# A feed-forward layer with two plain blocks in place of four and ten Strassen pairs in place of nine, the first pair's weights prepared ahead of the token sums

## The chip, the cores and the metric

The kernel runs on one core of one Trainium2 chip. The metric is the device time in microseconds (us) of one execution. Before the change the median of three runs is 1004.85 us (1004.83 to 1004.9). The rows below come from one further execution that was taken with a profile: it took 1005.55 us, of which 1003.8 us lie between the first and the last instruction (its span).

## The reference

One decoder layer for 576 tokens of width 1024: 512 tokens of a prompt and 64 of eight short samples. A mixing part (convolution, recurrence and attention to a memory, joined by gates) comes first; the change is in the feed-forward part behind it, whose inner width D_FF is 2816:

```python
h = _rmsnorm(x, norm_pre_ffn)
f = jax.nn.silu(jnp.einsum('bld,df->blf', h, w_ffn_gate)) * jnp.einsum('bld,df->blf', h, w_ffn_up)
f = jnp.einsum('blf,fd->bld', f, w_ffn_down)
x = x + _rmsnorm(f, norm_post_ffn)
```

All inputs and outputs are fp32, and the result is wanted close to fp32 accuracy.

## The kernel before

**Three matmuls for one product.** Every operand of a product is split into a high and a low part (`split`, L99: the high part is a rounded copy by ScalarE on L102, or L105 where a scale goes with it; the low part is the difference, by VectorE on L103 or L106). `mm3` (L93) then issues three TensorE matmuls, high by high (L95), high by low (L96), low by high (L97). So each weight and each activation costs one instruction of ScalarE and one of VectorE before TensorE can use it.

**The feed-forward part** handles the 2816 inner columns as 22 blocks of 128 columns. `h2` holds the normalised tokens, high and low, as 8 blocks of 128 rows (the k blocks, along the 1024 of the width) by 576 tokens. `ffn_norm(ti)` writes it for one token tile: PE turns four blocks at a time into one PSUM bank (L1179), then ACT and DVE split each (L105, L106, 128x128 each). Token tiles 0 and 1 (tokens 0 to 255) come last. The next steps are:

- `ffn_group(f, w, g)` (L1197), a *plain* block: for block f and token group g (0: tokens 0 to 255; 1: tokens 256 to 575) 8 x 3 matmuls for the gate and as many for the up weights, each with a PSUM bank of its own; ACT's sigmoid (L1201) and two DVE multiplications (L1202, L1204) empty the banks. The two groups have 256 and 320 columns.
- `sprep(m)` and `smul(m, nxt)`, the *Strassen pairs*: two neighbouring blocks (256 columns) at once, as a 2 x 2 matrix of half width by half columns times a 2 x 2 matrix of half width by half tokens (288 each). Seven products in place of eight: 7 x 4 x 3 = 84 matmuls of 288 columns for the gate (m even) and as many for the up weights (m odd).
- The pairs need sums of the tokens: `token_sums_a` (L1223, tokens 288 to 575) and `token_sums_b` (L1232 for tokens 0 to 287, then L1234, L1236, L1237 and L1240 and four splits of 1152 elements; T0 to T3 are the split sums).
- They need sums of the weights too: `sprep(m)` loads 1 MB of raw weights (L1252) into one half of a ring of two, splits the quarter `a` (wa), makes four sums of 512 elements (L1269, L1270, L1276, L1277) and splits them and the quarters b and d (wq, 1024 elements each). `sprep` is a generator: each `next` goes to the following `yield`.
- The down projection follows behind the last pair.

**What sets the order.** The kernel is traced in program order, and the framework then orders each engine's queue by a simulation of its own; an engine works its queue strictly as it stands. Weights loaded by `ffn_w` (L1194) come from SP's queue, as do the raw weights and the write-back of the residual to DRAM (`spill`, L1358). PSUM gives four banks named mm and four named sd; a product can begin only when a bank of its name is free. With `LEAD = 4`, blocks 0 to 3 are plain and blocks 4 to 21 are nine pairs (m = 0 to 17). Blocks 0 and 1 are done for group 1, then `token_sums_a`, then blocks 0 and 1 for group 0, then `token_sums_b`, then blocks 2 and 3; `sprep(0)` is begun in block 3.

Of the kernel before, what the change touches and what calls it, by code (L numbers as in the profile page):

```python
# [27 lines left out]

WARM = 14

LEAD = 4

HELD = (2, 5)

# [8 lines left out]
def tile_decoder_layer(  # L43
# [19 lines left out]
    def nm(s):  # L63
        seq[0] += 1
        return f"{s}_{seq[0]}"

    def big(dt=F32, n=4608):
        return pS.tile([P, n], dt, tag="S", name=nm("S"))
# [7 lines left out]
    def mtmp(n=576, dt=F32):  # L76
        return pt.tile([P, n], dt, tag="mt", name=nm("mt"), bufs=2)
# [13 lines left out]
    def f32(ap):  # L91
        return ap.bitcast(F32)
# [6 lines left out]
    def split(hi, lo, src, scale=None, eng=None):  # L99

        if scale is None:
            A.activation(hi, src, AF.Copy)  # L102
            (eng or V).tensor_tensor(lo, src, f32(hi), op=ALU.subtract)  # L103
        else:
            ins = A.activation(hi, src, AF.Identity, scale=scale)  # L105
            ins2 = V.scalar_tensor_tensor(out=lo, in0=src, scalar=scale, in1=f32(hi), op0=ALU.mult,  # L106
                                          op1=ALU.subtract)
            return ins, ins2

    def wprep(src, k, c, hi=None, lo=None, eng=None):  # L110
        raw = pw.tile([P, k, c], F32, tag="wr", name=nm("wr"), bufs=3)
        nc.sync.dma_start(raw, src.rearrange("(k p) c -> p k c", p=P))
        if hi is None:
            hi = pw.tile([P, k, c], FR, tag="wh", name=nm("wh"), bufs=3)
            lo = pw.tile([P, k, c], FR, tag="wl", name=nm("wl"), bufs=3)
        split(hi, lo, raw, eng=eng)
        return hi, lo

    def proj(w, col, act, b0, nk, groups=(0, 1)):

        res = []
        whi, wlo = w
        ahi, alo = act
        for g in groups:
            t0, n = GRP[g]
            ps = mmb()
            for k in range(nk):
                mm3(ps[:, :n], whi[:, k, col:col + P], wlo[:, k, col:col + P],
                    ahi[:, b0 + k, t0:t0 + n], alo[:, b0 + k, t0:t0 + n], k == 0, k == nk - 1)
            res.append((ps, t0, n))  # L130
        return res
# [160 lines left out]
    def wcols(w, c, n=P):  # L292
        return w[0][:, c:c + n], 8 if w.shape[1] == D else w.shape[1] // P, n
# [895 lines left out]
    def hid(f):  # L1189
        while len(hids) <= f // 8:  # L1190
            hids.append(big().rearrange("p (f t) -> p f t", f=8))
        return hids[f // 8][:, f % 8]

    def ffn_w(f, eng=None):  # L1194
        return tuple(wprep(*wcols(w, P * f), eng=eng) for w in (w_ffn_gate, w_ffn_up))

    def ffn_group(f, w, g):  # L1197
        hf = hid(f)
        (ps, t0, n), = proj(w[0], 0, h2, 0, 8, (g,))
        sg = mtmp(320)  # L1200
        A.activation(sg[:, :n], ps[:, :n], AF.Sigmoid)  # L1201
        V.tensor_tensor(sg[:, :n], ps[:, :n], sg[:, :n], op=ALU.mult)  # L1202
        (ps, t0, n), = proj(w[1], 0, h2, 0, 8, (g,))
        V.tensor_tensor(hf[:, t0:t0 + n], ps[:, :n], sg[:, :n], op=ALU.mult)  # L1204
# [21 lines left out]
    def tsplit(i, src):  # L1226
        split(xT["hl"][0][:, i], xT["hl"][1][:, i], src)

    def token_sums_b():
        r = xT["r"]  # L1230
        hi, lo = (x[:, :, TH[1]] for x in h2)
        V.tensor_tensor(r[:, :, TH[1]], f32(hi), f32(lo), op=ALU.add)  # L1232
        b11, b12, b21, b22 = (r[:, 4 * k:4 * k + 4, TH[t]] for k in range(2) for t in range(2))
        V.tensor_tensor(b11, b11, b12, op=ALU.subtract)  # L1234
        tsplit(0, b11)
        V.scalar_tensor_tensor(out=b12, in0=b12, scalar=-1.0, in1=b22, op0=ALU.mult, op1=ALU.add)  # L1236
        V.scalar_tensor_tensor(out=b22, in0=b22, scalar=-1.0, in1=b11, op0=ALU.mult, op1=ALU.subtract)  # L1237
        tsplit(1, b22)
        tsplit(2, b12)
        V.scalar_tensor_tensor(out=b21, in0=b22, scalar=-1.0, in1=b21, op0=ALU.mult, op1=ALU.subtract)  # L1240
        tsplit(3, b21)
# [3 lines left out]
    def sprep(m):  # L1245

        p, w = LEAD // 2 + m // 2, (w_ffn_gate, w_ffn_up)[m % 2]
        d = sw[m] = {}
        if "t" not in rawring:
            rawring["t"] = big()  # L1250
        raw = rawring["t"][:, 2048 * (m % 2):2048 * (m % 2) + 2048].rearrange("p (k i c) -> p k i c", k=8, i=2)
        nc.sync.dma_start(raw.rearrange("p k i c -> p k (i c)"),  # L1252
                          w[0][:, 256 * p:256 * p + 256].rearrange("(k p) c -> p k c", p=P))
        yield
        a, c = raw[:, 0:4, 0], raw[:, 0:4, 1]
        b, dd = raw[:, 4:8, 0], raw[:, 4:8, 1]
        wa = px.tile([P, 2, 4, P], FR, tag="x", name=nm("wa"))
        split(wa[:, 0], wa[:, 1], a)
        d["a"] = (wa[:, 0], wa[:, 1])
        yield  # L1260

        def sums():
            return pw.tile([P, 2, 4, P], F32, tag="wr", name=nm("ws"), bufs=3)

        def places(pool, t0, t1):
            return tuple(pool.tile([P, 2, 4, P], FR, tag=t, name=nm("wq"), bufs=5 if t == "x" else 3) for t in (t0, t1))

        s1 = sums()
        V.tensor_tensor(s1[:, 0], c, dd, op=ALU.add)  # L1269
        V.tensor_tensor(s1[:, 1], a, c, op=ALU.add)  # L1270
        q = places(px, "x", "x")
        split(q[0], q[1], s1)
        d["cd"], d["ac"] = ((q[0][:, i], q[1][:, i]) for i in range(2))
        yield
        s2 = sums()
        V.tensor_tensor(s2[:, 0], s1[:, 0], a, op=ALU.add)  # L1276
        V.tensor_tensor(s2[:, 1], s2[:, 0], b, op=ALU.add)  # L1277
        q = places(pw, "wh", "wl")
        split(q[0], q[1], s2)
        d["acd"], d["abcd"] = ((q[0][:, i], q[1][:, i]) for i in range(2))  # L1280
        yield
        q = places(pw, "wh", "wl")
        q4 = tuple(x.rearrange("p i k c -> p k i c") for x in q)
        split(q4[0], q4[1], raw[:, 4:8])
        d["b"], d["d"] = ((q[0][:, i], q[1][:, i]) for i in range(2))
        yield
# [5 lines left out]
    def smul(m, nxt):  # L1292

        p, up = LEAD // 2 + m // 2, m % 2
        d = sw.pop(m)
# [88 lines left out]
    token_sums_a()  # L1384
    for f in range(2):
        ffn_group(f, wf[f], 0)
    token_sums_b()
    sw = {}
    NM = NF - LEAD
    nxt = None  # L1390
    for f in range(2, LEAD):
        w = ffn_w(f)
        ffn_group(f, w, 1)
        if f == LEAD - 1:
            nxt = sprep(0)
            next(nxt)
        ffn_group(f, w, 0)
    for _ in nxt:
        pass
    for m in range(NM):  # L1400
        nxt = sprep(m + 1) if m + 1 < NM else iter(())
# [153 lines left out]
```

## Time and profile before

| | before |
|---|---|
| median of 3 runs | 1004.85 us (1004.83 to 1004.9) |
| the profiled execution | 1005.55 us, span 1003.8 us |
| PE (TensorE matmul) busy | 986.9 us, 98% of the span |
| DVE (VectorE) busy | 693.3 us, 69% |
| ACT (ScalarE) busy | 433.5 us, 43% |
| mean granted TensorE clock | 0.997 of 2.4 GHz |

The busy times are sums over the whole span, so they tell which engine is scarce on average; the stage that the change touches runs from 617 to 656 us, and is read on its own below. A time in a row of the timeline is counted from the span's start. PE's matmuls are pipelined: the time that one costs is the distance from its start to the start of the next, not its length in the row.

### The profile page before, as it was taken

How to read it: one execution, taken by the hardware profiler on the slowest of the kernel's cores; microseconds unless marked ns; L12 is line 12 of the kernel's file. 1: busy time of each engine (PE TensorE's matmuls, PEld its weight loads, DVE VectorE, ACT ScalarE, POOL GpSimd, SP SyncE). 2: the span in 40 equal slices, each digit the busy share in tenths (PEclk: the TensorE clock that was granted, in tenths of full speed). 3: DMA queues.
4: the chain of work that ended last, by engine and by line, in shares of the span. 5: the costliest groups of instructions: out<-in, count | busy, mean ns of one | idle time of the engine just before them, and what ended most of it. 6: DMA issues, size and time to landing. Idle time of an engine off the chain costs nothing.

```text
span 1003.8 us, 16880 instructions
## 1 busy us (share of the span) xinstructions
PE 986.9 (98%) x6915; PEld 924.0 (92%) x6915; DVE 693.3 (69%) x1235; ACT 433.5 (43%) x766; POOL 33.5 (3%) x127
## 2 busy tenths in 40 slices
PE   8999999999899999999999999999999999999997
PEld 7997899889699999999999779999999999999995
DVE  6689997485875365566548788878777876813715
ACT  6544346574621232223234466344444544614612
POOL 1120000000101001001000000000000000000000
PEclk9999999999999999999999999999999999999999
DMA  8415421543743222222323615023232333321302
GB/s 244 140 64 194 121 80 47 148 132 107 207 134 95 84 85 75 76 87 65 95 77 134 181 64 178 1 85 114 77 104 85 96 115 137 139 81 54 128 20 95
DMA packets 125931, 106.55 MB, mean 106 GB/s; under 512 B 3208, under 2 KB 110244, under 8 KB 125846
## 3 DMA queue, kind: packets, MB, share of 16 engines
q1 hardware_dynamic: 125854, 105.48, 33.9%
q8 instruction: 54, 0.88, 0.4%
q14 instruction: 23, 0.19, 0.1%
HBM read 97.15 MB, written 8.68 MB: 105 GB/s over the span
## 4 chain that ended last, share of the span: by engine, by line
PE 82%; DVE 7%; DMA 5%; ACT 2%; issue 2%; POOL 1%; SPq 0%; DVEq 0%; ACTq 0%
PE mm L96 18%; PE mm L95 18%; PE mm L97 18%; PE sd L96 3%; PE sd L95 3%; PE sd L97 3%; PE sd L1465 2%; PE sd L1466 2%; PE sd L1467 2%; DVE wl L103 1%; DMA x<-in_cache_mem_v_dram 1%; DMA wr<-in_w_ffn_gate_dram 1%; DVE S L428 1%; DMA wr<-in_w_out_dram 1%; DVE S L106 1%
## 5 line engine op out<-in xcount | busy, mean ns | idle before, releaser
L96 PE MATMUL mm<-S,wh 128*128 128x320 f32 (+1 forms) x1216 | 363.3, 299 | 0.3 <-DVE S L106 0.3
L95 PE MATMUL mm<-S,wh 128*128 128x320 f32 (+1 forms) x1216 | 361.5, 299 | 1.5 <-ACT S L105 1.0
L97 PE MATMUL mm<-S,wl 128*128 128x320 f32 (+1 forms) x1216 | 362.4, 299 | 0.0
L95 PEld LDWEIGHTS mm<-S,wh 128*128 128x128 f32 x1216 | 227.9, 188 | 6.5 <-issue 2.6
L97 PEld LDWEIGHTS mm<-S,wl 128*128 128x128 f32 x1216 | 228.3, 188 | 3.9 <-issue 3.5
L96 PEld LDWEIGHTS mm<-S,wh 128*128 128x128 f32 x1216 | 228.6, 188 | 3.6 <-issue 1.5
L103 DVE TENSOR_TENSOR wl<-wr,wh 128x1024 fp32r<-128x1024 f32 x98 | 119.6, 1221 | 127.9 <-ACT wh L102 127.5
L102 ACT ACTIVATE wh<-wr 128x1024 fp32r<-128x1024 f32 x98 | 103.6, 1059 | 224.9 <-PE mm L96 174.1
L428 DVE SCALAR_TENSOR_TENSOR S<-S,cT,S 128x512 f32<-128x512 f32 x120 | 89.9, 749 | 2.5
L96 PE MATMUL mm<-S,wq 128*128 128x288 f32 x216 | 63.7, 295 | 0.0
L97 PE MATMUL mm<-S,wq 128*128 128x288 f32 x216 | 63.7, 295 | 0.0
L96 PE MATMUL sd<-S,wq 128*128 128x288 f32 x216 | 63.6, 295 | 0.0
L95 PE MATMUL sd<-S,wq 128*128 128x288 f32 x216 | 63.6, 294 | 0.0
L95 PE MATMUL mm<-S,wq 128*128 128x288 f32 x216 | 63.6, 294 | 0.0
L97 PE MATMUL sd<-S,wq 128*128 128x288 f32 x216 | 63.1, 294 | 0.0
L102 ACT ACTIVATE wq<-ws 128x1024 fp32r<-128x1024 f32 x36 | 37.9, 1056 | 37.8 <-PE mm L96 35.2
L103 DVE TENSOR_TENSOR wq<-ws,wq 128x1024 fp32r<-128x1024 f32 x36 | 43.7, 1217 | 3.0 <-ACT wq L102 3.0
L103 DVE TENSOR_TENSOR S<-S,S 128x1152 fp32r<-128x1152 f32 (+3 forms) x46 | 44.1, 986 | 1.8 <-ACT S L102 1.7
L102 ACT ACTIVATE S<-S 128x1152 fp32r<-128x1152 f32 (+3 forms) x46 | 38.1, 864 | 6.9 <-DVE S L521 4.9
L97 PEld LDWEIGHTS mm<-S,wq 128*128 128x128 f32 x216 | 40.6, 188 | 0.0
L96 PEld LDWEIGHTS sd<-S,wq 128*128 128x128 f32 x216 | 40.5, 188 | 0.0
L95 PEld LDWEIGHTS sd<-S,wq 128*128 128x128 f32 x216 | 40.5, 188 | 0.0
(371 smaller groups left out, 1689.5 us busy)
## 6 DMA issues: line engine op xcount, KB each, us to landing
wr<-in_w_in_dram SPq DMA_DIRECT2D x52, 512.0 KB
wr<-in_w_ffn_down_dram SPq DMA_DIRECT2D x22, 512.0 KB
S<-in_w_ffn_gate_dram SPq DMA_DIRECT2D x9, 1024.0 KB
S<-in_w_ffn_up_dram SPq DMA_DIRECT2D x9, 1024.0 KB
x<-in_x_prompt_dram SPq DMA_DIRECT2D x8, 512.0 KB
wr<-in_w_mem_kv_dram SPq DMA_DIRECT2D x8, 512.0 KB
x<-in_cache_mem_k_dram SPq DMA_DIRECT2D x8, 512.0 KB
x<-in_cache_mem_v_dram SPq DMA_DIRECT2D x8, 512.0 KB
```

The lines of the kernel that those rows point to most:

```text
L95: T.matmul(out, lhsT=whi, rhs=xhi, start=start, stop=False, skip_group_check=more)
L96: T.matmul(out, lhsT=whi, rhs=xlo, start=False, stop=False, skip_group_check=more)
L97: last["mm"] = T.matmul(out, lhsT=wlo, rhs=xhi, start=False, stop=stop, skip_group_check=more)
L102: A.activation(hi, src, AF.Copy)
L103: (eng or V).tensor_tensor(lo, src, f32(hi), op=ALU.subtract)
L106: ins2 = V.scalar_tensor_tensor(out=lo, in0=src, scalar=scale, in1=f32(hi), op0=ALU.mult, op1=ALU.subtract)
L428: queue(V.scalar_tensor_tensor(out=dp, in0=src, scalar=w, in1=dp, op0=ALU.mult, op1=ALU.add))
L1465: T.matmul(pa[ti], lhsT=ah, rhs=w[0][:, kk, :], start=f == 0, stop=False)
L1466: T.matmul(pa[ti], lhsT=al, rhs=w[0][:, kk, :], start=False, stop=False)
L1467: T.matmul(pa[ti], lhsT=ah, rhs=w[1][:, kk, :], start=False, stop=f == NF - 1)
```

## The change

Two blocks that were plain (2 and 3) become a tenth pair. The preparation of the first pair's weights is traced ahead of `token_sums_b`: one `next` issues the load, the second splits the quarter `a`.

```diff
-LEAD = 4
+LEAD = 2
...
     token_sums_a()
     for f in range(2):
         ffn_group(f, wf[f], 0)
+    sw = {}
+    nxt = sprep(0)
+    next(nxt)
+    next(nxt)
     token_sums_b()
-    sw = {}
     NM = NF - LEAD
-    nxt = None
-    for f in range(2, LEAD):
-        w = ffn_w(f)
-        ffn_group(f, w, 1)
-        if f == LEAD - 1:
-            nxt = sprep(0)
-            next(nxt)
-        ffn_group(f, w, 0)
     for _ in nxt:
         pass
     for m in range(NM):
```

What the framework makes of it is seen in the queues. In the rows below S_5800 and S_5801 are the high and low part of `h2`; sd_6376 and sd_6391 are PSUM banks with turned blocks of token tile 0, sd_6426 and sd_6441 with those of token tile 1. S_6686 is the ring of raw weights of the changed kernel, ws are sums of weights, wa and wq their splits, S_6574 the token sums, S_6576 and S_6577 their high and low parts. mm_6578, mm_6606 (block 0) and mm_6632, mm_6660 (block 1) are the banks of gate and up for group 0.

**First place: DVE, between the first splits of tokens 0 to 255 and the token sums** (a piece of the difference, + is the changed kernel; a little earlier stand, also new, L1269, L1270 and the split wa_6688 of the gate weights).

```order
+L1276 TENSOR_TENSOR ws_6711<-ws_6704,S_6686 128x512
 L106 SCALAR_TENSOR_TENSOR S_5801<-sd_6426,gT,S_5800 128x128
+L1269 TENSOR_TENSOR ws_6784<-S_6686 128x512
+L1270 TENSOR_TENSOR ws_6784<-S_6686 128x512
+L103 TENSOR_TENSOR wq_6708<-ws_6704,wq_6707 128x1024
+L103 TENSOR_TENSOR wa_6754<-S_6686,wa_6754 128x512
+L1277 TENSOR_TENSOR ws_6711<-ws_6711,S_6686 128x512
 L106 SCALAR_TENSOR_TENSOR S_5801<-sd_6441,gT,S_5800 128x128
 L106 SCALAR_TENSOR_TENSOR S_5801<-sd_6426,gT,S_5800 128x128
+L1276 TENSOR_TENSOR ws_6807<-ws_6784,S_6686 128x512
+L103 TENSOR_TENSOR wq_6715<-ws_6711,wq_6714 128x1024
+L1277 TENSOR_TENSOR ws_6807<-ws_6807,S_6686 128x512
```

Before, the last nine L106 stand behind one another; now twelve instructions on weights stand among them: eight sums (four for m = 0, four for m = 1), two splits wa and two splits wq. Behind the last row shown come the last two L106 and L1232.

**Second place: DVE, the token sums** (a piece of the difference).

```order
 L1232 TENSOR_TENSOR S_6574<-S_5800,S_5801 128x8x288
 L1234 TENSOR_TENSOR S_6574<-S_6574 128x4x288
-L103 TENSOR_TENSOR wl_6708<-wr_6705,wh_6707 128x1024
+L103 TENSOR_TENSOR wq_6719<-S_6686,wq_6718 128x4x2x128
 L1202 TENSOR_TENSOR mt_6603<-mm_6578,mt_6603 128x256
 L1236 SCALAR_TENSOR_TENSOR S_6574<-S_6574 128x4x288
-L103 TENSOR_TENSOR wl_6822<-wr_6819,wh_6821 128x1024
+L103 TENSOR_TENSOR wq_6811<-ws_6807,wq_6810 128x1024
+L1202 TENSOR_TENSOR mt_6657<-mm_6632,mt_6657 128x256
 L1204 TENSOR_TENSOR S_6464<-mm_6606,mt_6603 128x256
 L103 TENSOR_TENSOR S_6577<-S_6574,S_6576 128x1152
```

The order of the token sums stays: L1232, L1234, a split of weights, L1202 that frees the bank mm_6578, and so on; splits of Strassen weights take the places of splits of plain weights.

**Third place: PE, the end of group 0 and what follows it.** Before:

```order
L95 MATMUL mm_6660<-S_5800,S_6345 128x256
L96 MATMUL mm_6660<-S_5801,S_6345 128x256
L97 MATMUL mm_6660<-S_5800,S_6345 128x256
L95 MATMUL mm_6711<-S_5800,wh_6701 128x320 [waits DVE_49]
L96 MATMUL mm_6711<-S_5801,wh_6701 128x320
```

and in the changed kernel:

```order
L96 MATMUL mm_6578<-S_5801,wh_5804 128x256 [waits DVE_49]
L97 MATMUL mm_6578<-S_5800,wl_5805 128x256
L96 MATMUL mm_6606<-S_5801,wh_5810 128x256
L97 MATMUL mm_6606<-S_5800,wl_5811 128x256
L96 MATMUL mm_6632<-S_5801,S_6345 128x256
L97 MATMUL mm_6632<-S_5800,S_6345 128x256
L96 MATMUL mm_6660<-S_5801,S_6345 128x256
L97 MATMUL mm_6660<-S_5800,S_6345 128x256
L95 MATMUL mm_6722<-S_5800,wa_6688 128x288 [waits DVE_49]
```

Before, the four banks of group 0 are finished one after another and block 2 follows; now all four are kept open to the last split block, and the next product is X of the first pair (mm_6722), which waits for L1202 to free a bank of the name mm.

## Rows read from the trace of the kernel before

**Rows 1.** The page, busy time of each engine, share of the span, instructions.

```profile
PE 986.9 (98%) x6915; PEld 924.0 (92%) x6915; DVE 693.3 (69%) x1235; ACT 433.5 (43%) x766; POOL 33.5 (3%) x127
```

**Rows 2.** Stretches: window, length, busy (count) PE PEld DVE ACT POOL, PEclk, DMA share, GB/s.

```profile
617.10:628.60 11.50, 11.50 (x99) 11.50 (x97) 10.19 (x16) 6.35 (x13) 0.00 (x0) 1.00 0.20 64
628.60:655.60 27.00, 27.00 (x206) 27.00 (x205) 22.54 (x31) 10.33 (x14) 0.00 (x0) 1.00 0.01 1
670.00:850.00 180.00, 180.00 (x1358) 180.00 (x1357) 145.10 (x222) 87.69 (x137) 0.00 (x0) 1.00 0.31 100
```

**Rows 3.** PE's waits, whole span, the longest: us in total, times, longest.

```profile
PE sd L204 <- POOL ident masks.py:199: 1.8, 1, 1.8
```

**Rows 4.** Timeline of PE: start us, us, what; group 0 starts, ends, first pair starts.

```profile
617.08 0.48 PE L95 MATMUL mm<-S,wh 128*128 128x256 f32 x2
...
628.51 0.28 PE L97 MATMUL mm<-S,S 128*128 128x256 f32 x1
628.63 0.31 PE L95 MATMUL mm<-S,wh 128*128 128x320 f32 x1
628.78 0.31 PE L96 MATMUL mm<-S,wh 128*128 128x320 f32 x1
...
655.68 0.29 PE L95 MATMUL mm<-S,wa 128*128 128x288 f32 x1
```

**Rows 5.** PE by form, 628.6 to 655.6 us: busy, mean ns, idle before.

```profile
L96 PE MATMUL sd<-S,wq 128*128 128x288 f32 x4 | 1.2, 294 | 0.0
```

**Rows 6.** Timeline of DVE, 617 to 630 us: last splits of tokens, then token sums.

```profile
616.93 0.49 DVE L1204 TENSOR_TENSOR S<-mm,mt 128x320 f32<-128x320 f32 x1
617.34 1.38 DVE L106 SCALAR_TENSOR_TENSOR S<-sd,gT,S 128x128 fp32r<-128x128 f32 x5
...
620.46 0.35 DVE L106 SCALAR_TENSOR_TENSOR S<-sd,gT,S 128x128 fp32r<-128x128 f32 x1 [0.43 <-ACT S L105]
620.85 2.56 DVE L1232 TENSOR_TENSOR S<-S,S 128x2304 f32<-128x2304 f32 x1
623.44 1.36 DVE L1234 TENSOR_TENSOR S<-S 128x1152 f32<-128x1152 f32 x1
...
626.40 0.42 DVE L1202 TENSOR_TENSOR mt<-mm,mt 128x256 f32<-128x256 f32 x1
626.73 1.35 DVE L1236 SCALAR_TENSOR_TENSOR S<-S 128x1152 f32<-128x1152 f32 x1
628.00 1.22 DVE L103 TENSOR_TENSOR wl<-wr,wh 128x1024 fp32r<-128x1024 f32 x1
629.13 0.42 DVE L1204 TENSOR_TENSOR S<-mm,mt 128x256 f32<-128x256 f32 x1
```

**Rows 7.** DVE by form, 656 to 860 us: busy, mean ns, idle before and releaser.

```profile
L103 DVE TENSOR_TENSOR wq<-ws,wq 128x1024 fp32r<-128x1024 f32 x34 | 41.3, 1217 | 3.0 <-ACT wq L102 3.0
L1276 DVE TENSOR_TENSOR ws<-ws,S 128x512 f32<-128x512 f32 x16 | 10.9, 681 | 0.0
L103 DVE TENSOR_TENSOR wa<-S,wa 128x512 fp32r<-128x512 f32 x16 | 10.9, 681 | 0.0
```

**Rows 8.** Timeline of SP's queue, 606 to 613 us: write-backs, first raw gate and up.

```profile
606.94 2.88 SPq L1358 DMA_DIRECT2D x<-x  x4
609.93 1.19 SPq L1252 DMA_DIRECT2D S<-in_w_ffn_gate_dram  x1
611.16 1.36 SPq L1252 DMA_DIRECT2D S<-in_w_ffn_up_dram  x1
```

**Rows 9.** Stretches as in rows 2, about the end of these loads.

```profile
617.00:619.00 2.00, 2.00 (x20) 2.00 (x18) 1.82 (x7) 1.51 (x6) 0.00 (x0) 1.00 1.07 346
619.00:620.00 1.00, 1.00 (x10) 1.00 (x10) 0.82 (x3) 0.48 (x2) 0.00 (x0) 1.00 0.21 58
```

**Rows 10.** Stretches as in rows 2, at the end of the span.

```profile
998.00:1000.00 2.00, 0.00 (x0) 0.00 (x0) 1.65 (x8) 0.29 (x1) 0.00 (x0) 1.00 0.00 0
1000.00:1002.00 2.00, 0.00 (x0) 0.00 (x0) 0.65 (x1) 0.00 (x0) 0.00 (x0) 0.55 0.58 218
```

## The prediction

> **What bounds the kernel now.** I read the busy times first: PE is busy 98% of the span, DVE 69%, ACT 43% [rows 1]. So on average every matmul taken away is time gained. But the change acts in one stage, so the stretches come next. From 617.1 to 628.6 us (blocks 0 and 1, tokens 0 to 255) PE is busy all 11.50 us and DVE 10.19 of them; from 628.6 to 655.6 us PE 27.00 and DVE 22.54 of 27.00; in the middle of the pairs, 670 to 850 us, PE 180 and DVE 145 of 180 [rows 2]. PE never waits there, and DVE has 1.3 us free in the first stretch, 4.5 in the second. That is what to watch: PE is the bound, with DVE close behind exactly where the change puts work.
>
> **What is removed and added on PE.** Two plain blocks go: 2 x 48 matmuls of 320 columns at 628.78 - 628.63 = 0.15 us and 2 x 48 of 256 columns at 628.63 - 628.51 = 0.12 us [rows 4], 25.9 us. The trace gives it more exactly: from 628.63 to the first product of the pair at 655.68 are 27.05 us [rows 4], in which 12 matmuls of the first pair also ran (4 on each of three lines, one shown [rows 5]). One matmul of a pair costs 180.0 / 1358 = 0.1326 us [rows 2], so those 12 are 1.6 us and the two blocks 25.45 us. One more pair is 2 x 84 = 168 matmuls, 22.3 us. Gain on PE: 25.45 - 22.3 = **3.1 us**. SP loses the four 512 KB loads of plain weights; no transfer of importance runs from 628.6 to 655.6 us (1 GB/s [rows 2]), so I put that at nothing. DVE and ACT lose four weight splits and eight bank-emptying steps and gain the work of two more `sprep` calls. From 650 us on DVE's spare time in the pairs (35 of 180 us) covers this.
>
> **What is moved on DVE, the first stall.** In the changed order twelve instructions on weights stand among the last splits of tokens 0 to 255. Eight sums of 512 elements at 0.68, two splits wa at 0.68 and two splits wq at 1.22 us [rows 7] make 9.2 us. Neighbours overlap a little: the 1.35 us of L1236 gave way after 1.27 [rows 6], 0.08 each, so 8.3 us remain. The split of token blocks itself costs 1.38 / 5, about 0.26 us, nine of them 2.3. Before, DVE took up these nine at 617.34 and was done at 620.81, with waits for ACT between them [rows 6]. Now it is done at 617.34 + 2.3 + 8.3 = about 628.0, with some semaphore latency 628.3, which is 7.5 us later.
>
> PE meets this in the middle of group 0. ACT makes the high parts of the same splits, in the same mixed order; with 6.35 of 11.5 us busy [rows 2] it is the earlier of the two, and I price DVE alone. Group 0 starts at 617.08 [rows 4] and has 40 matmuls that need none of the late blocks: 40 x 0.12 = 4.8 us, to 621.9. The 41st needs a split (sd_6426) that stands behind nine of the twelve inserted instructions and seven of the nine token splits: 617.34 + (6 x 0.68 + 2 x 0.68 + 1.22 - 9 x 0.08) + 7 x 0.26 = 625.1 us. So PE idles some 3.2 us. The other 56 matmuls take 6.7, and group 0 ends at 631.8 in place of 628.6. The very last split, at 628.3, is no longer in the way: it is asked for at about 630.9.
>
> **The second stall, a bank.** Next on PE is X of the first pair. It needs a bank of the name mm, and all four are held by group 0 until L1202 empties the first. L1202 stands on DVE behind L1232 (2.59 us to the next start), L1234 (1.27, as for L1236) and one weight split (628.00 to 629.13, 1.13) [rows 6]: 628.3 + 2.6 + 1.3 + 1.1 + 0.35 = 633.7, and X starts at about 633.9. PE idles another **2.1 us**. L1232 cannot start earlier, since it reads all the splits.
>
> **The rest of the first pair.** Behind L1202 DVE still has three sums and four splits of 1152 elements at 1.27 each and three weight splits at 1.13, mixed with bank work; PE's first pair asks for them in order. Laid out in the same durations, T0's low part is there at 638.1 (in time: 638.6 asked for), T1's high part about 0.3 late, the split wq for `ac` about 1.3 late, T1's low part about 1.0 late. **2.5 us** together. After that DVE is ahead again.
>
> Sum: 3.2 + 2.1 + 2.5 = 7.8 us of idle PE against 3.1 gained, +4.7 us. The profiled execution's 1005.55 would become 1010.25; it stands 0.7 above the median of the runs, so on the median's scale 1004.85 + 4.7 = **1009.6 us**. The stalls were never in the trace of before, so bounds: from below no stall at all (-3.1 us; what the sum would be if DVE's order did not bind), from above the late data and the slower clock below. I take 7.8 because each part of it rests on strict queue orders and on durations that repeat to some hundredths.
>
> **Where the load stands.** DVE's first inserted instruction needs the raw gate weights. The load is issued at 609.93, behind four write-backs, and the up weights at 611.16 [rows 8]; in the changed queue of SP both keep this place, since only the loads of plain weights ahead of them go. The transfers go on at 346 GB/s until 619 and at 58 in the microsecond after [rows 9]. The up weights are the last 1.05 MB, 3 us at that speed; so the gate's would end at about 616.4 and the up's at 619.5. DVE asks for the first at 617.6 and for the second at 621: just in time, at no cost.
>
> **The clock.** A matmul-free stretch from 998 to 1000 us was still granted 1.00, and the next two microseconds 0.55, a mix of 2.4 and 1.2 GHz [rows 10]; one wait of 1.8 us is the longest that the kernel has elsewhere [rows 3]. So idle time of PE does bring the clock down here, though only after more than 2 us of it; the first stall, 3.2 us, lies between, and I count no loss. The Trainium skill, TensorE: Matmul & The Clock Gate, section "Part 1: The HAM clock gate", calls the throttled state the default, which only activity lifts; it speaks against a change that opens gaps in a PE that had none. By it the sum would be that of the clock rival below; the trace bears it out only at the kernel's end.
>
> **Rivals.**
> - *The order does not bind and the 3.1 us are kept: 1004.85 - 3.1 = 1001.7 us, faster.* DVE would have to deliver the split that PE asks for at 621.9 by then and L1202 by 629. For it: over the whole stretch DVE's work fits (69% on average), and the weight work is only moved forward, so later on DVE has less. Against it: 8.3 us of inserted work in a stretch with 1.3 us free. It decides by where the last split of tokens ends: up to 622 us PE is never late, at 628 it is. 0.09.
> - *Only one stall, or shorter ones: about 3 us of idle time against 3.1 gained, 1004.8 us, no change.* If the first stall is real but the bank is free when PE asks (L1202 before 631.8), and the rest is hidden. Against it: L1232 alone starts at 628.3. 0.09.
> - *The gate's weights land late.* If gate and up share the DMA engines rather than follow one another, both end near 620; DVE and ACT stand from 617.6 to 620 with the token splits queued behind: +2.4 us, 1012.0 us. For it: both are queued within 1.3 us. 0.12.
> - *The clock falls in the first stall.* The 56 matmuls behind it then take twice 0.12 each as long as it stays at 1.2 GHz. Group 0 would end up to 6.7 us later, at 638.5, of which 2.1 are covered by the wait for the bank: +4.6 us, 1014.2 us. 0.08.
>
> **How the numbers follow.** My forecast, with its own range of 1006.5 to 1011.5 for the sizes of the stalls, has 0.62. The range that should hold the time 8 times in 10 reaches to the case of no change below and nearly to the clock's case above, 1004.0 to 1013.5; it leaves out the faster case (0.09) and most of the clock's (0.08). A difference under 0.2%, 2.0 us, I take as what can't be told from no change. Faster by more: 0.09, within it: 0.09, slower: 0.82.
>
> **What would show it.** In the changed profile PE should show, for the first time, idle time of about 3 us near 622 to 625 us, ended by DVE's split on L106; about 2 us more before the first matmul with wa, ended by L1202; and two or three waits of 0.3 to 1.3 us up to 645, ended by L103 and L102. L1232 should start near 628 in place of 620.85. From the first wa product to the down phase there should be ten times 22.3 us with no further wait. The forecast is wrong if L1232 starts before 623 us or if PE shows no idle time between 617 and 645; it is wrong the other way if L1269 waits for its DMA, or if the granted clock shows less than 1.00 there.

## The result, and the profile after

The changed kernel takes 1011.51 us (median of three runs, 1011.47 to 1011.84) against 1004.85 us: 6.7 us slower, ratio 1.0064 with a 95% interval of 1.0046 to 1.0082. The profiled execution is the median one, 1011.51 us, span 1009.8 us.

The waits of PE from 600 to 670 us, where before there was none in the stretches of [rows 2] (engine, line, what it waited for: us in total, times, longest):

```profile
PE mm L96 <- DVE S L106: 3.0, 2, 2.4
PE mm L95 <- DVE mt L1202: 1.9, 1, 1.9
PE mm L96 <- DVE S L103: 0.6, 1, 0.6
```

They are the forecast stalls in their order: splits of tokens, the bank that L1202 frees, the low part of a token sum. One stretch answers to [rows 2] for the whole stage (columns as there):

```profile
616.00:650.00 34.00, 28.42 (x195) 27.55 (x194) 32.17 (x43) 16.71 (x27) 0.00 (x0) 0.90 0.13 44
```

PE is busy 28.42 of 34 us and DVE 32.17. The mean granted clock is 0.90. Before, in the same part of the stage, DVE was nearly as full and PE never waited:

```profile
618.00:652.00 34.00, 34.00 (x265) 34.00 (x264) 30.29 (x41) 14.52 (x22) 0.00 (x0) 1.00 0.04 13
```

So DVE's share alone doesn't make it the bound. What has changed is that PE now asks at once for what DVE is still making. DVE's timeline shows it (start, length, what), to be held against [rows 6]:

```profile
622.20 0.69 DVE L1277 TENSOR_TENSOR ws<-ws,S 128x512 f32<-128x512 f32 x1
622.80 0.61 DVE L106 SCALAR_TENSOR_TENSOR S<-sd,gT,S 128x128 fp32r<-128x128 f32 x2
623.32 0.68 DVE L1276 TENSOR_TENSOR ws<-ws,S 128x512 f32<-128x512 f32 x1
624.01 1.23 DVE L103 TENSOR_TENSOR wq<-ws,wq 128x1024 fp32r<-128x1024 f32 x1
625.15 0.69 DVE L1277 TENSOR_TENSOR ws<-ws,S 128x512 f32<-128x512 f32 x1
...
626.53 0.35 DVE L106 SCALAR_TENSOR_TENSOR S<-sd,gT,S 128x128 fp32r<-128x128 f32 x1 [0.44 <-ACT S L105]
626.92 2.56 DVE L1232 TENSOR_TENSOR S<-S,S 128x2304 f32<-128x2304 f32 x1
629.51 1.36 DVE L1234 TENSOR_TENSOR S<-S 128x1152 f32<-128x1152 f32 x1
632.20 1.22 DVE L103 TENSOR_TENSOR wq<-S,wq 128x1024 fp32r<-128x1024 f32 x1 [1.32 <-ACT wq L102]
633.34 0.41 DVE L1202 TENSOR_TENSOR mt<-mm,mt 128x256 f32<-128x256 f32 x1
```

The splits (L106) at 622.8 stand between weight sums and splits, L1232 starts at 626.92 in place of 620.85, and L1202 at 633.34 in place of 626.40. L1202 stood behind more than DVE's own work: DVE was idle for 1.32 us in front of it, waiting for a split on ACT that could start only when PE was done with a matmul of group 0 (L96). So a late end of group 0 makes the bank late too. ACT's row:

```profile
631.11 1.06 ACT L102 ACTIVATE wq<-S 128x1024 fp32r<-128x1024 f32 x1 [4.61 <-PE mm L96]
```

PE's timeline over the first and the second stall:

```profile
620.68 0.39 PE L95 MATMUL mm<-S,S 128*128 128x256 f32 x2
623.46 0.52 PE L96 MATMUL mm<-S,wh 128*128 128x256 f32 x1 [2.38 <-DVE S L106]
623.77 0.42 PE L97 MATMUL mm<-S,wl 128*128 128x256 f32 x1
623.99 0.42 PE L95 MATMUL mm<-S,wh 128*128 128x256 f32 x1
...
631.63 0.28 PE L97 MATMUL mm<-S,S 128*128 128x256 f32 x1
633.81 0.61 PE L95 MATMUL mm<-S,wa 128*128 128x288 f32 x1 [1.89 <-DVE mt L1202]
634.21 0.44 PE L96 MATMUL mm<-S,wa 128*128 128x288 f32 x1
634.45 0.44 PE L97 MATMUL mm<-S,wa 128*128 128x288 f32 x1
```

Behind each stall a matmul takes longer: 623.99 - 623.77 = 0.22 us for 256 columns in place of 0.12, and 0.24 for 288 in place of 0.13. The stretches say why:

```profile
622.00:624.00 2.00, 0.54 (x3) 0.54 (x4) 2.00 (x5) 1.08 (x2) 0.00 (x0) 0.89 0.00 0
624.00:626.00 2.00, 2.00 (x11) 2.00 (x11) 1.99 (x4) 0.23 (x1) 0.00 (x0) 0.50 0.00 0
634.00:636.00 2.00, 2.00 (x9) 2.00 (x10) 2.00 (x2) 1.65 (x2) 0.00 (x0) 0.50 0.61 198
```

The granted clock was 0.50 there, 1.2 GHz in place of 2.4, once after the first stall and once after the second. Mind what a busy share hides: PE is "busy" all 2.00 us from 624 to 626, with 11 matmuls in place of 17.

**The account.** I took PE's timeline from the first matmul of group 0 to the kernel's last one and sorted each distance between starts: up to what its width usually takes (0.119 us for 256 columns, 0.147 for 320, 0.1326 for 288, 0.2345 for 512), a wait where the row names one, or a slow step (over 0.06 us longer and no wait named). Before: 378.99 us with no waits and 0.7 of slow steps. After: 385.80 with 6.2 of waits and 4.3 of slow steps. Without both, 378.3 and 375.3: the pair in place of two blocks does gain 3.0 us, and 9.8 are lost. Of the other two differences in the spans, one goes the other way: group 0 starts at 615.17 in place of 617.08. Of this 1.0 us stands already at 545 us, ahead of the work that the change touches, and the start differs from profile to profile (615.1 to 617.6 us). The other is at the end. From the start of the last matmul to the end of the span pass 8.83 us in place of 7.73, and only after the change the DMA rows of the last 3 us show a load of instructions (queue, kind: packets, MB, share of 16 DMA engines' time):

```profile
q14 instruction: 1, 0.01, 0.6%
```

So 6.8 - 1.9 + 1.1 = 6.0 us between the two spans.

### The profile page after: what moved, and what is told of

Same layout as the page of the kernel before. It is cut to its first block, busy times and chain, and to the rows that moved or that the text cites. A ratio compares the mean times of both kernels' runs of the same rounds, so it can differ in the third digit from the quotient of the medians.

```text
span 1009.8 us, 16850 instructions
## 1 busy us (share of the span) xinstructions
PE 987.0 (98%) x6891; PEld 923.8 (91%) x6891; DVE 702.7 (70%) x1251; ACT 439.8 (44%) x775; POOL 33.5 (3%) x127
## 4 chain that ended last, share of the span: by engine, by line
PE 87%; DVE 5%; DMA 4%; ACT 2%; issue 1%; SPq 0%; DVEq 0%; ACTq 0%
PE mm L96 19%; PE mm L97 18%; PE mm L95 18%; PE sd L97 3%; PE sd L96 3%; PE sd L95 3%; PE sd L1460 2%; PE sd L1461 2%; PE sd L1462 2%; DMA x<-in_cache_mem_v_dram 1%; DVE S L103 1%; PE mm L1150 1%; PE mm L1149 1%; PE mm L1151 1%; DMA wr<-in_w_out_dram 1%
## 5 line engine op out<-in xcount | busy, mean ns | idle before, releaser
L96 PE MATMUL mm<-S,wh 128*128 128x320 f32 (+1 forms) x1152 | 345.5, 300 | 3.3 <-DVE S L106 3.3
L97 PE MATMUL mm<-S,wl 128*128 128x320 f32 (+1 forms) x1152 | 344.4, 300 | 0.0
L95 PE MATMUL mm<-S,wh 128*128 128x320 f32 (+1 forms) x1152 | 342.8, 300 | 1.2 <-ACT S L105 1.0
L96 PEld LDWEIGHTS mm<-S,wh 128*128 128x128 f32 x1152 | 217.4, 189 | 7.0 <-DVE S L106 3.9
L95 PEld LDWEIGHTS mm<-S,wh 128*128 128x128 f32 x1152 | 216.4, 189 | 6.0 <-issue 2.6
L97 PEld LDWEIGHTS mm<-S,wl 128*128 128x128 f32 x1152 | 217.3, 189 | 4.0 <-issue 3.5
L103 DVE TENSOR_TENSOR wl<-wr,wh 128x1024 fp32r<-128x1024 f32 x94 | 114.8, 1222 | 127.6 <-ACT wh L102 127.4
L96 PE MATMUL mm<-S,wq 128*128 128x288 f32 x240 | 71.0, 296 | 0.6 <-DVE S L103 0.6
L97 PE MATMUL mm<-S,wq 128*128 128x288 f32 x240 | 70.7, 295 | 0.0
L96 PE MATMUL sd<-S,wq 128*128 128x288 f32 x240 | 70.7, 295 | 0.0
L95 PE MATMUL mm<-S,wq 128*128 128x288 f32 x240 | 70.6, 294 | 0.0
L95 PE MATMUL sd<-S,wq 128*128 128x288 f32 x240 | 70.5, 295 | 0.0
L97 PE MATMUL sd<-S,wq 128*128 128x288 f32 x240 | 70.1, 295 | 0.0
L103 DVE TENSOR_TENSOR wq<-ws,wq 128x1024 fp32r<-128x1024 f32 x40 | 48.7, 1216 | 2.9 <-ACT wq L102 2.5
L96 PEld LDWEIGHTS mm<-S,wq 128*128 128x128 f32 x240 | 45.0, 188 | 0.9 <-DVE S L103 0.9
L95 PEld LDWEIGHTS sd<-S,wq 128*128 128x128 f32 x240 | 45.2, 189 | 0.0
L96 PEld LDWEIGHTS sd<-S,wq 128*128 128x128 f32 x240 | 45.1, 188 | 0.0
L97 PEld LDWEIGHTS mm<-S,wq 128*128 128x128 f32 x240 | 45.1, 188 | 0.0
```

Source lines behind the costliest of these rows:

```text
L95: T.matmul(out, lhsT=whi, rhs=xhi, start=start, stop=False, skip_group_check=more)
L96: T.matmul(out, lhsT=whi, rhs=xlo, start=False, stop=False, skip_group_check=more)
L97: last["mm"] = T.matmul(out, lhsT=wlo, rhs=xhi, start=False, stop=stop, skip_group_check=more)
```

## The experiments

Two theories at first. A: DVE has too much to do from the token splits to the end of the first pair once two blocks of cover are gone; an order only moves the stalls. B: the order is the loss, weight work ahead of the token splits. The table has the medians and, from the profiled execution of each, the account from the start of group 0 (waits and slow steps as above).

| run | us (ratio to before, interval) | waits | slow | to the last matmul |
|---|---|---|---|---|
| before | | 0.0 | 0.7 | 378.99 |
| the change | 1011.51 (1.0046 to 1.0082) | 6.2 | 4.3 | 385.80 |
| sums first | 1012.46 (1.0057 to 1.0088) | 8.7 | 3.0 | 387.00 |
| four plain blocks | 1005.34 (0.999 to 1.001) | 0.0 | 0.7 | 379.17 |
| splits first | 1009.79 (1.0034 to 1.0071) | 7.3 | 5.3 | 387.63 |
| weight sums on POOL | 1011.21 (1.0047 to 1.0077) | 8.1 | 2.7 | 386.00 |
| no weight sums | 1007.40 (1.0013 to 1.0032) | 5.7 | 2.6 | 383.42 |
| nor low parts of T | 1004.70 (0.9985 to 1.0004) | 2.1 | 2.8 | 380.06 |
| order by hand | 1016.80 (1.0098 to 1.0129) | 9.1 | 6.2 | 390.78 |
| the change again | 1012.92 (1.0068 to 1.0093) | 6.1 | 4.1 | 385.61 |
| filled gap | 1011.38 (1.0055 to 1.0082) | 6.5 | 1.4 | 384.68 |
| relieved and ordered | 1005.95 (1.0004 to 1.0024) | 3.7 | 3.3 | 382.26 |
| tokens' sum on ACT | 1010.87 (1.0044 to 1.0078) | 6.4 | 2.5 | 384.07 |

Before took 1004.61 to 1005.37 us beside these runs. An account is of one execution, and that can lie off the median: the profiled one of the splits first took 1013.29 us, its other three 1008.75 to 1009.87. With no weight sums it lies 0.6 us above the median, without the low parts too 1.8, and relieved and ordered 2.8.

**Fewer blocks without the early weights.**

```diff
+    token_sums_b()
     sw = {}
     nxt = sprep(0)
     next(nxt)
     next(nxt)
-    token_sums_b()
```

> Two plain blocks and ten pairs as in the changed kernel, but the first pair's load and split are traced behind the token sums again. Theory A (DVE has no free time between 612 and 651 us, so an order only moves the stalls; what costs is that two plain blocks of cover are gone): the token splits end at about 619 us, but the first product's weights (wa) come behind all the token sums, at about 633 to 635; PE, done with group 0 at 626.8, idles about 8 us there and 4 to 6 more in the pair: 1012 to 1018 us. Theory B (the loss comes from weight work that stands ahead of the token splits): the loss is gone, 1002 to 1005 us.

Measured 1012.46 us. The token splits are on time and PE runs through group 0, and then it waits for what now comes later:

```profile
PE mm L95 <- ACT wa L102: 3.3, 2, 2.6
PE sd L95 <- ACT wq L102: 2.9, 1, 2.9
PE sd L97 <- DVE wq L103: 1.5, 2, 1.2
```

The waits are shorter than I expected (8.7 in all, not 12 to 14), but as A says they have moved, not gone: from 626 to 644 us DVE is busy 18.00 of 18 us. B falls in its plain form.

**The early weights without fewer blocks.**

```diff
-LEAD = 2
+LEAD = 4
...
     NM = NF - LEAD
+    for f in range(2, LEAD):
+        w = ffn_w(f)
+        ffn_group(f, w, 1)
+        ffn_group(f, w, 0)
```

> Four plain blocks and nine pairs as before the change, only the first pair's load and split are traced ahead of the token sums. Theory A: the cover of two plain blocks (25 us of PE work) is there, nothing waits: 1004 to 1006 us, as before. Rival C (the early preparation itself costs, whatever covers it): some 2 us or more above before, 1006.5 to 1009 us.

Measured 1005.34 us, ratio 1.000, and PE shows no wait between 612 and 670 us. Tracing the first weights early costs and brings nothing where 25 us of plain blocks cover DVE; the loss belongs to the blocks taken away.

**Token splits ahead of the weight work** (that of m = 0).

```diff
-    next(nxt)
+    with tc.issue_after(last["h2"][0].ins), tc.issue_after(last["h2"][1].ins):
+        next(nxt)
     token_sums_b()
...
-    for _ in nxt:
-        pass
+    with tc.issue_after(last["h2"][0].ins), tc.issue_after(last["h2"][1].ins):
+        for _ in nxt:
+            pass
```

> The changed kernel with one order imposed: all work on the first pair's weights m = 0 is queued behind the last token split on ACT and DVE. Theory A: the first stall (about 623 us) goes, the same DVE work is then missing later: PE waits 3 to 4 us for T0, 2 to 3 for b and d, 3 for T1: 1008 to 1013 us. Theory B: 1001.7 to 1005 us.

Measured 1009.79 us. The first stall is gone, and in its place PE waits for the low parts of the token sums:

```profile
PE mm L96 <- DVE S L103: 2.8, 1, 2.8
PE sd L96 <- DVE S L103: 1.8, 1, 1.8
```

and its stretch of the stage (columns as above) is

```profile
616.00:650.00 34.00, 27.84 (x192) 26.36 (x191) 33.21 (x46) 16.49 (x26) 0.00 (x0) 0.90 0.16 52
```

DVE is busy 33.2 of 34 us, which leaves an order little to gain. But these rows are of the slowest of four executions, 3.5 us above the median. By the medians this one is worth 1.7 us, of which 1.1 are the shorter end (its profile has no load of instructions there).

**The eight sums on POOL** (L1269, L1270, L1276 and L1277 on GpSimd for m = 0 and 1; they stand one line further down there).

```diff
+        E = G if m < 2 else V
         s1 = sums()
-        V.tensor_tensor(s1[:, 0], c, dd, op=ALU.add)
+        E.tensor_tensor(s1[:, 0], c, dd, op=ALU.add)
...
```

> The changed kernel with the eight weight sums of m = 0 and 1 on POOL in place of DVE; nothing else. Theory A: DVE is relieved of 8 x 0.6 = 4.8 us in the stage that it bounds; if POOL takes no longer than about 1.2 us for a sum, the time falls by 3 to 5 us to 1006 to 1009 us. If POOL is slow (over 2 us a sum) the splits wq that need the sums come late and the time stays at 1010 to 1014 us. Theory B: the three weight splits that still stand among the token splits cost 2.5 us of PE's wait less the 3.1 gained: 1003 to 1006 us.

Measured 1011.21 us, the case of a slow POOL. POOL's timeline:

```profile
619.95 2.19 POOL L1270 TENSOR_TENSOR ws<-S 128x512 f32<-128x512 f32 x1
...
623.80 3.60 POOL L1278 TENSOR_TENSOR ws<-ws,S 128x512 f32<-128x512 f32 x1
```

and DVE's in the same us:

```profile
622.99 3.27 DVE L1232 TENSOR_TENSOR S<-S,S 128x2304 f32<-128x2304 f32 x1
628.52 1.23 DVE L103 TENSOR_TENSOR wq<-ws,wq 128x1024 fp32r<-128x1024 f32 x1 [2.27 <-ACT wq L102]
629.67 2.42 DVE L1234 TENSOR_TENSOR S<-S 128x1152 f32<-128x1152 f32 x1
```

A sum takes 1.3 to 3.6 us on POOL against 0.68 on DVE, and while POOL works, L1232 takes 3.27 us in place of 2.56 and L1234 2.42 in place of 1.36: the two slow each other down. DVE then waits 2.27 us for a late sum, and PE 6.2 us for T0. The run says nothing against A, since DVE was hardly relieved: from 616 to 650 us it was busy 30.51 us in place of 32.17.

**DVE relieved by leaving work out.** First the eight weight sums, then the four low parts of the token sums as well.

```diff
+        if m < 2:
+            s1 = raw[:, 0:4].rearrange("p k i c -> p i k c")
...
+        if m < 2:
+            split(q[0], q[1], raw[:, 4:8].rearrange("p k i c -> p i k c"))
...
```

and, in the second run,

```diff
-        xT["hl"] = [big(FR).rearrange("p (c k t) -> p c k t", c=4, k=4) for _ in range(2)]
+        xT["hl"] = [big(FR).rearrange("p (c k t) -> p c k t", c=4, k=4)] * 2
...
-        split(xT["hl"][0][:, i], xT["hl"][1][:, i], src)
+        A.activation(xT["hl"][0][:, i], src, AF.Copy)
```

> The changed kernel without the eight weight sums of m = 0 and 1 (raw quarters are split in their place, so the first pair's products are not the reference's); every split and every matmul is kept. Theory A (DVE's total work from the last token splits to the end of the first pair sets PE's idle time): 8 x 0.6 = 4.8 us less on DVE, the idle time falls by about as much and the clock stays up more: 1004.5 to 1007.5 us. Rival D (PE waits for ACT's high parts, for PSUM banks or for the loads as much as for DVE): less than 2 us gained, 1009 to 1011 us.

> As the run without weight sums, and the four low parts of the token sums are left out too (the high part is read in their place), 4 x 1.27 = 5.1 us less on DVE, 9.9 us in all; all matmuls are kept. Theory A: hardly any idle time of PE is left, and the gain of 3.1 us of PE work shows: 1001.5 to 1003.5 us. If the 3.1 us were mis-sized, the time stays at 1004 us or more though PE does not wait.

Measured 1007.40 and 1004.70 us; the second missed its range by 1.2 us. From the start of group 0 to the last matmul 4.8 us less on DVE brought 2.4 us and 9.9 less 5.7 (385.80 to 383.42 and 380.06): A's direction, with somewhat over half its size. By the medians it is 4.1 and 6.8 us, of which 1.1 are the shorter end in both. PE's waits in the second run:

```profile
PE mm L95 <- ACT S L105: 1.2, 2, 1.0
PE mm L96 <- DVE S L106: 0.7, 1, 0.7
```

No wait is left behind group 0, where DVE's total bound; what is left are the token splits, now behind weight splits on ACT as well, and 1.6 us of slow steps behind them. This part fits B, so that both theories would hold, each for one stall; the next run tests it.

**Both together**: that second run with the weight work of m = 0 and 1 behind the token splits.

```diff
+    def held(gen):
+        for _ in range(5):
+            with tc.issue_after(last["h2"][0].ins), tc.issue_after(last["h2"][1].ins):
+                next(gen, None)
+            yield
...
```

> As the run without weight sums and without low parts of the token sums (9.9 us less on DVE), and the weight work of m = 0 and 1 is queued behind the last token split on ACT and DVE; all matmuls are kept. That run still had 2.0 us of PE waits at 619 to 623 us, for splits of tokens that stood behind weight splits on ACT, and 2.3 us of a slower clock behind them. Theory A with the first stall put down to the order: both go, and the whole gain of 3.1 us shows: 1001.5 to 1002.7 us. If ACT or the banks take over as the bound: 1003.5 us or more.

Measured 1005.95 us: a miss. In the stage itself PE waits only twice, 1.1 us in all, with the clock at 1.00:

```profile
616.00:650.00 34.00, 32.94 (x256) 32.49 (x255) 29.43 (x45) 21.33 (x38) 0.00 (x0) 1.00 0.29 94
```

but the gain doesn't reach the end. In the pairs DVE now waits 36.4 us for raw weights from 660 us on, in the changed kernel 14.8, and in the profiled execution PE runs into that at 745.9 us, 1.8 us and slow steps behind it. What came late on DVE:

```profile
739.15 0.69 DVE L1275 TENSOR_TENSOR ws<-S 128x512 f32<-128x512 f32 x1 [3.38 <-DMA S<-in_w_ffn_up_dram]
```

and the stretch behind PE's wait, with the clock at 0.50:

```profile
747.00:749.00 2.00, 2.00 (x10) 2.00 (x10) 1.28 (x2) 0.00 (x0) 0.00 (x0) 0.50 0.96 311
```

That load was issued at 732.65, 6.5 us earlier, when its half of the ring came free. So with little lost in front, the load of the raw weights is close to being the next bound. But this execution took 2.8 us more than the median; how much of the median's miss comes from here isn't shown. Whether a third half would give the rest back wasn't tried.

**The order by hand.** Every step of ACT and DVE for m = 0 and 1 and the token sums was queued behind the one before, in the order in which PE asks; m = 2 behind them.

```diff
+    for step in (w0, w0, ts, ts, w0, w1, w0, ts, ts, w0, w1, w1, ts, ts, w1, w1):
+        with tc.issue_after(behind[0]), tc.issue_after(behind[1]):
+            next(step)
...
```

> The changed kernel with ACT's and DVE's whole order from the last token split to the end of the first pair fixed by hand, in the order in which PE asks: wa, two sums, token sums and T0, cd and ac, wa of m = 1, acd and abcd, T1, b and d, then m = 1, T2, T3, and m = 2 behind that. Theory A: DVE has some 29 us of work from 619 us on and PE 30 us from then to the end of the pair, so even a good order leaves several short waits: 1004 to 1008 us, better than the changed kernel by 3 us or more and no better than before by more than 1. Theory B (order alone is the loss): 1001.7 to 1003.5 us.

Measured 1016.80 us, the slowest of all. A strict order on both engines makes each wait for the other:

```profile
PE mm L95 <- ACT S L102: 2.3, 1, 2.3
PE mm L95 <- ACT wq L102: 1.6, 1, 1.6
```

ACT waited 4.0 us for L1240, a token sum far back in DVE's queue, with weight splits ready behind it. The framework's own order is the better one here. The 1004 to 1008 us expected were a miss, and this run tells nothing of a lower limit.

**The clock.** 14 matmuls of 256 columns into a free bank, queued where the first stall was; the changed kernel again beside it.

```diff
+                    first = T.matmul(args[0], lhsT=args[1], rhs=args[3], start=False, stop=False)
+                    with tc.issue_after(first.ins):
+                        f1 = last["filler"](14)
...
```

> The changed kernel once more, as the base for the run with filler matmuls on the same chip: 1.0055 to 1.0075 of before.

> The changed kernel with 14 more matmuls of 256 columns (1.7 us) into a free PSUM bank, queued on PE where its first stall was (2.4 us before the split of sd_6426); their result is not read, DVE's and ACT's orders are those of the changed kernel. Reading E: the clock stays at 1.00 after the gap, group 0 ends about 1.6 us earlier, ACT's split of b and d, which waits for group 0's weights to come free, and with it L1202 come 1.3 us earlier, and the rest of the clock's loss was covered by the waits for DVE: 1.0 to 1.6 us less than the changed kernel. If the slower clock cost its whole 3.3 us: 3 us or more less. If it was covered by DVE's queue altogether: within 0.4 us of the changed kernel.

Measured 1012.92 us for the change (ratio 1.0080, a little above what was expected) and 1011.38 with the gap filled, 1.5 us less; the intervals overlap, so by time alone it isn't settled. The trace is clearer: the clock stayed at 1.00 in the whole stage,

```profile
616.00:650.00 34.00, 28.72 (x216) 27.19 (x215) 32.96 (x45) 16.82 (x28) 0.00 (x0) 1.00 0.17 54
```

although the second stall, 2.0 us, was still there; in the run relieved and ordered, a wait of 1.76 us with no other near it was followed by 0.50, so the length of a wait alone doesn't settle whether the clock falls. And from the start of group 0 to the last matmul are 384.68 us in place of 385.61. Slow steps fell by 2.7 us, and the end came 0.9 earlier. As far as one execution each shows, most of the slow matmuls ran while PE would have waited anyway.

**The tokens' sum on ACT**, with the splits first; nothing is left out.

```diff
+                if ti < 2:
+                    A.activation(hids[2][:, kk, c0:c0 + P], ps[:, n * k:n * k + n], AF.Identity,
+                                 scale=gT[:, 8 + kk:9 + kk])
...
-        V.tensor_tensor(r[:, :, TH[1]], f32(hi), f32(lo), op=ALU.add)
+        V.tensor_tensor(r[:, :, 256:HT], f32(hi)[:, :, 256:], f32(lo)[:, :, 256:], op=ALU.add)
```

> The run with the token splits first, all of the computation kept; ACT writes the unsplit tokens 0 to 255 itself (16 instructions of 128x128 from PSUM, 0.27 us each), so that L1232 shrinks from 2304 to 256 elements and DVE loses 2.3 us in the stage. Theory A: PE's idle time falls by about 2 us and the clock stays up more: 1006 to 1008.5 us against 1009.8 for the splits first. If ACT's 4.3 us more delay the splits of tokens: 1009.5 us or more.

Measured 1010.87 us, the case of late splits. ACT is full in exactly those us (8.0 of 8 from 616 to 624), and DVE waits 4.0 us for its high parts:

```profile
DVE S L106 <- ACT S L105: 4.0, 12, 1.9
```

No version here beats the kernel before.

## Why the prediction was right, and where its sum was not

The time fell within the range, 1.9 us above the forecast and just past the forecast's own range of 1006.5 to 1011.5. Step by step:

- **The gain of 3.1 us** is there: 378.3 against 375.3 us without waits and slow steps, 3.0.
- **The first stall**, 3.2: measured 0.66 + 2.38 = 3.0 us, ended by L106 at 619.4 and 623.46. The whole stage starts 1.9 us earlier than I had it, so PE asked earlier for the split, and the split came 1.6 us earlier. That group 0 still ended at 631.8, as forecast, is luck: the slow matmuls behind the stall, which the sum left out, took 1.6 us.
- **The second stall**, 2.1: measured 1.9, ended by L1202. This is luck in part as well. L1232 started at 626.92 for the expected 628.3, but then DVE waited 1.32 us for ACT, which the sum put at nothing, and L1202 came at 633.34 as forecast. Of the 628.3, 0.3 us were put down to semaphore latency; no row shows so much: in both traces L1232 starts 0.04 us behind the end of the last split (620.46 + 0.35 to 620.85, and 626.53 + 0.35 to 626.92).
- **The rest of the pair**, 2.5: measured 0.6, one wait for T1's low part in place of three. This term was mis-sized, and with the next one it belongs together.
- **The clock**, "I count no loss": the step that failed, by the prediction's own sign, a granted clock under 1.00 in this stage. I read from [rows 3, 10] that a gap of about 2 us leaves the clock alone. The trace of the kernel before speaks against it in a place that no row above shows: the clock was at 0.50 from 260 to 262 us, where PE had worked 2.0 of the 4 us ahead and waited at most 1.2 us at once (PE's longest wait from 250 to 264 us, then stretches as in [rows 2]).

```profile
PE sd L489 <- DVE tb L487: 1.2, 1, 1.2
258.00:260.00 2.00, 1.21 (x14) 0.63 (x16) 2.00 (x3) 1.45 (x4) 0.00 (x0) 0.88 0.02 4
260.00:262.00 2.00, 2.00 (x44) 1.86 (x40) 2.00 (x8) 1.99 (x3) 0.00 (x0) 0.50 0.73 221
```

In the changed kernel the clock fell to 0.50 behind the first stall (2.38 us, with 0.66 a little earlier) and behind the second (1.89), and the slow steps cost 3.6 us more than before. Some 2 of these seem to have taken only the place of waits, which may be why the third term came out small; about 1 us was net, by the filled gap. The Trainium skill, TensorE: Matmul & The Clock Gate, "Part 1: The HAM clock gate", calls the throttled state the default, which activity lifts. The trace agrees: 0.50 from 624 to 626 us behind an idle PE, and 1.00 again from 628 to 630. But my price for the rival, up to 4.6 us, was too high: it took all 56 matmuls behind the first stall as slow, and only 16 were.
- **Not foreseen**: 1.1 us at the very end. The three profiles of the changed program (the two of the change and the filled gap, which only adds matmuls) show an instruction load in the last 3 us and 8.8 us from the last matmul to the end; of the other kernels' profiles none shows the load there, and their tail is 7.7 to 8.0 us. It goes with the program's layout; which engine fetched, and whether the load alone is the cause, wasn't tried.
- **The raw loads** came in time, as worked out: DVE's first sum of weights ran at 615.81 without a wait for them. Only ACT waited, 0.85 us for the up weights, at 619.06.

So the forecast of 4.7 us over before was 7.8 - 3.1; what was measured between the profiles is 9.8 - 3.0 from group 0 on, less 1.9 of an earlier start and 1.1 more at the end. The nearness to the total owes something to terms that cancel.

The cause in one sentence: the two plain blocks were not only slower work for PE, they were the 25 us in which DVE made the token sums and the first pair's weights, and without them PE asks for these while DVE, busy 32 of 34 us, is still at them, and waits.

## What to carry to other kernels

Before replacing slow work of the bound engine by faster work, add up what the other engines finish behind it. Here DVE was busy 22.5 of the 27 us of that stretch, and the gain of 3 us was paid back twice over as waits. Show first whether order or total is the limit: reorder once, and leave work out once; if the waits only move, it is the total. And a PE that begins to wait, even for 2 us, may come back at half clock, as it did here, so a stall can cost more than its length, but less where another wait stands behind it. Look for the clock's low stretches in the whole trace before counting on it.

## What was not expected of the hardware

- Vector sums on POOL and on DVE slow each other: 128x512 sums took 1.3 to 3.6 us on POOL, and DVE's 1152-element sum went from 1.36 to 2.42 us beside them.
- The clock fell behind a wait of 1.89 us in one run and behind a lone one of 1.76 us in another, and stayed at 1.00 behind one of 2.0 us in a third, where the gap before it had been filled.
- A load of instructions among the last transfers goes with an end that is 1.1 us later.
